# Windowed attention on one core: TensorE's 32 written-out units turned into one loop with hand-made semaphores and single q, k, v buffers

## Chip, cores and metric

The kernel runs on one core of one Trainium2 chip. The metric is the device time of one execution in microseconds (us). Kernels that were timed in the same rounds ran on the same chip, beside runs of the kernel before.

## The reference, cut

q, k and v are float32 of shape (4, 4096, 1536). Each sequence is cut into windows of 64 rows, and attention is taken inside each window.

```python
def reference(q, k, v):
    B, S, D = q.shape                      # 4, 4096, 1536
    W = 64; nw = S // W; scale = D ** -0.5
    q_w, k_w, v_w = (x.reshape(B, nw, W, D) for x in (q, k, v))
    logits = np.einsum('bnwd,bnud->bnwu', q_w, k_w) * scale
    ...                                    # softmax over the last axis
    out = np.einsum('bnwu,bnud->bnwd', attn, v_w)
    return out.reshape(B, S, D).astype(np.float32)
```

There are 302 MB to read and 100.7 MB to write, and little arithmetic for each byte.

## The kernel before

The 16,384 rows are worked on in 32 units of 512. A unit loads q, k and v (3 MB of float32 each, cast to fp16 on the way in), transposes q and k on TensorE, forms the scores, takes the exponent on ScalarE, multiplies by v, divides by the row sums while copying out of PSUM, and stores 3 MB. Loads and stores are issued by GpSimd, but for the first q and the last three pieces of the output, which SyncE issues. q and k have two buffers and v has three, so loads run two or three units ahead. The last unit is cut into three parts, so that its last pieces are small.

```python
    units = [Unit(i * UR, [(0, 4, 2)]) for i in range(N - 1)]
    units.append(Unit((N - 1) * UR, [(0, 2, 2), (2, 3, 1), (3, 4, 1)]))
    qkp = ctx.enter_context(tc.tile_pool(name="qkp", bufs=2))
    vp = ctx.enter_context(tc.tile_pool(name="vp", bufs=3))
    outp = ctx.enter_context(tc.tile_pool(name="outp", bufs=3))
    ...
    for ui, u in enumerate(units):
        for i in range(len(u.parts)):
            last = ui == N - 1 and i == len(u.parts) - 1
            blocks = scores(u, i)              # transposes, products, exponent
            if i == 0:
                load_all(ui + 2, "qk")         # two units ahead
            for h, et in blocks:
                values(u, i, h, et, last)
            if not last:
                store(u, i)
        load_all(ui + 3, "v")                  # three units ahead
```

All of this is written out by Python: TensorE's program holds 32 copies of a unit.

The softmax here doesn't subtract the row's maximum and nothing guards it: scores larger than these inputs give would overflow.

## Time and profile before

| | before |
|---|---|
| time, median (3 runs) | 947.19 us (946.93 to 947.67) |
| span of the profiled run | 945.3 us |
| busy: TensorE, VectorE, ScalarE | 70%, 33%, 34% |
| DMA, software queue | 100.3% of 16 engines' span |

Lines of the profile page of the kernel before. The row of slices gives the busy share of 40 equal slices in tenths; the queue lines give packets, MB and the share of 16 DMA engines' span.

```profile
span 945.3 us, 10170 instructions
PE 662.5 (70%) x4088; PEld 449.4 (48%) x4088; DVE 315.2 (33%) x554; ACT 318.6 (34%) x612; POOL 83.7 (9%) x139
...
DMA  9999999999999999999999999999999999999997
...
q0 software_dynamic: 27232, 249.31, 100.3%
...
q8 instruction: 32, 0.52, 0.2%
q14 instruction: 15, 0.12, 0.0%
HBM read 301.99 MB, written 100.66 MB: 426 GB/s over the span
```

The DMA engines never rest until the last slice, and no compute engine is close to full. So the run is bound by moving bytes. Two more views of the same run follow. First, the waits of TensorE for loads (total, times, longest); then the order in which GpSimd issues its transfers after the first prefetch (start, duration, and in brackets the idle time of GpSimd before it and what ended it).

```profile
PE tp L147 <- DMA q<-in_q_dram: 70.7, 28, 3.8
PE tp L147 <- DMA k<-in_k_dram: 70.5, 30, 3.2
```

```profile
24.89 0.55 POOL L80 DMA_DIRECT2D q<-in_q_dram  x1 [19.41 <-PE tp L147]
31.74 0.54 POOL L80 DMA_DIRECT2D k<-in_k_dram  x1 [6.30 <-PE tp L147]
44.13 0.71 POOL L225 DMA_DIRECT2D out_dram<-out_sb  x1 [11.84 <-DVE xq L151]
44.83 0.72 POOL L80 DMA_DIRECT2D v<-in_v_dram  x1
```

q and k of unit 2 are issued at 25 and 32 us, long before the seven transfers of the start have landed (the last at 55 us).

A reading comes from the trace's completion records. A transfer is spread over 16 DMA engines, and each reports when it is done. The lag of an engine is how much later than the first of the 16 it reports. The engines drift apart:

```
kernel before         first of 16   last of 16   spread   sum of the 16 lags
first v (3rd)             24.59        25.41      0.82          4.6
61st transfer            448.27       451.76      3.49         25.9
119th transfer           871.17       876.90      5.73         45.2
last store               937.53       943.00      5.47         45.6
```

### The profile page before, as it was taken

To read this page: it belongs to the slowest core of one execution; us is meant where nothing else is said; L and a number is where in the kernel's file an instruction comes from. 1 tells how busy PE (TensorE), PEld (TensorE's weight loads), DVE (VectorE), ACT (ScalarE), POOL (GpSimd) and SP (SyncE) were. 2 spreads that over 40 slices of the span, in tenths; PEclk is the share of its full clock that TensorE was granted. 3 is DMA by queue.
4 is the path that set the end of the run, shared out by engine and by line. 5 is a ranking of instruction groups with operands and counts; after the bars stand their busy time and mean duration, and the time that the engine had idled before them with its cause. 6 is when DMAs were issued, how large, how long until landed. Compare 5 with 4: busy or idle time off the path is not lost. (4 is left out here: it accounts for less than half of the span.)

```text
span 945.3 us, 10170 instructions
## 1 busy us (share of the span) xinstructions
PE 662.5 (70%) x4088; PEld 449.4 (48%) x4088; DVE 315.2 (33%) x554; ACT 318.6 (34%) x612; POOL 83.7 (9%) x139
## 2 busy tenths in 40 slices
PE   2877777577766776767777677776677767676673
PEld 1555555345543544535455444554445534455442
DVE  2443234332333332333323333233332333332332
ACT  2443332333323332233332333323333233332342
POOL 1110010100101001010010100110100101001010
PEclk9998898998889999898987899798998798988998
DMA  9999999999999999999999999999999999999997
GB/s 260 216 228 267 281 281 281 242 258 283 282 281 253 247 282 283 280 263 240 280 282 279 273 236 274 282 282 276 240 266 283 280 278 248 255 283 281 281 251 325
DMA packets 27855, 253.89 MB, mean 269 GB/s; under 512 B 2208, under 2 KB 2208, under 8 KB 11808
## 3 DMA queue, kind: packets, MB, share of 16 engines
q0 software_dynamic: 27232, 249.31, 100.3%
q1 hardware_dynamic: 576, 3.93, 1.1%
q8 instruction: 32, 0.52, 0.2%
q14 instruction: 15, 0.12, 0.0%
HBM read 301.99 MB, written 100.66 MB: 426 GB/s over the span
## 5 line engine op out<-in xcount | busy, mean ns | idle before, releaser
L207 PE MATMUL o<-v,et 128*128 128x512 f16 x762 | 202.3, 377 | 50.6 <-ACT out_sb L216 34.2
L161 PE MATMUL lt<-xq,xk 128*128 128x256 f16 (+1 forms) x1536 | 225.7, 298 | 6.4 <-DVE xk L151 6.3
L147 PE MATMUL tp<-ident,q 128*128 128x128 f32 x768 | 142.6, 340 | 101.7 <-DMA q<-in_q_dram 70.7
L147 PE MATMUL tp<-ident,k 128*128 128x128 f32 x768 | 133.3, 312 | 72.3 <-DMA k<-in_k_dram 70.5
L161 PEld LDWEIGHTS <-xk 128*128 128x128 f16 x1536 | 155.5, 105 | 52.3 <-DVE xk L151 17.6
L147 PEld LDWEIGHTS tp<-ident,q 128*128 128x128 f32 x768 | 107.5, 173 | 143.3 <-issue 101.1
L216 ACT ACTIVATE out_sb<-o,rs 128x512 f32<-128x512 f32 x193 | 125.5, 685 | 101.5 <-PE o L207 100.7
L151 ACT COPY xk<-tp 128x512 f32<-128x512 f32 (+1 forms) x96 | 58.6, 610 | 275.2 <-PE tp L147 275.2
L151 DVE COPY xk<-tp 128x512 f32<-128x512 f32 (+1 forms) x97 | 66.9, 690 | 246.5 <-PE tp L147 246.5
L147 PEld LDWEIGHTS tp<-ident,k 128*128 128x128 f32 x768 | 106.4, 162 | 84.2 <-issue 77.0
L218 DVE TENSOR_SCALAR out_sb<-o,rs 128x512 f32<-128x512 f32 x191 | 137.6, 748 | 25.9 <-PE o L207 19.4
L151 DVE COPY xq<-tp 128x512 f32<-128x512 f32 (+1 forms) x129 | 86.7, 687 | 107.1 <-PE tp L147 104.2
L207 PEld LDWEIGHTS <-et 128*128 128x128 f16 x762 | 62.0, 96 | 112.8 <-issue 60.0
L187 ACT ACTIVATE et<-lt,zeros 32x128 f16<-32x128 f32 (+1 forms) x256 | 91.6, 358 | 35.3 <-PE lt L161 29.6
L151 ACT COPY xq<-tp 128x512 f32<-128x512 f32 x64 | 39.0, 609 | 189.3 <-PE tp L147 189.3
L211 DVE RECIPROCAL rs<-sp 128x1 f32<-128x1 f32 x128 | 21.6, 168 | 223.7 <-PE sp L205 223.7
L205 PE MATMUL sp<-ones,et 128*128 128x1 f16 x254 | 42.4, 167 | 40.6 <-ACT et L187 40.6
L205 PEld LDWEIGHTS <-et 128*128 128x128 f16 x254 | 24.4, 96 | 91.5 <-ACT et L187 50.1
L225 POOL DMA_DIRECT2D out_dram<-out_sb x33 | 23.2, 703 | 368.0 <-issue 331.2
L80 POOL DMA_DIRECT2D k<-in_k_dram x34 | 18.5, 544 | 307.6 <-PE tp L147 254.9
L80 POOL DMA_DIRECT2D q<-in_q_dram x33 | 17.9, 541 | 164.5 <-PE tp L147 144.1
L80 POOL DMA_DIRECT2D v<-in_v_dram x34 | 24.0, 708 | 6.6 <-DMA k<-in_k_dram 6.6
(12 smaller groups left out, 7.7 us busy)
## 6 DMA issues: line engine op xcount, KB each, us to landing
out_dram<-out_sb POOLq DMA_DIRECT2D x31, 3072.0 KB, 44.5
k<-in_k_dram POOLq DMA_DIRECT2D x31, 1536.0 KB, 49.6
v<-in_v_dram POOLq DMA_DIRECT2D x31, 1536.0 KB, 51.1
q<-in_q_dram POOLq DMA_DIRECT2D x30, 1536.0 KB, 52.9
raw<-in_q_dram SPq DMA_DIRECT2D x1, 3072.0 KB, 15.5
out_dram<-out_sb POOLq DMA_DIRECT2D x1, 1536.0 KB, 14.2
v<-in_v_dram POOLq DMA_DIRECT2D x1, 768.0 KB, 47.6
v<-in_v_dram POOLq DMA_DIRECT2D x2, 384.0 KB, 46.2
```

The lines of the kernel that those rows point to most:

```text
L80: nc.gpsimd.dma_start(out=dst, in_=rows(src, u.first[i], hi - lo, r))
L147: nc.tensor.transpose(tp[:, (c - c0) * R + r, j, :], pairs[:, c * P : (c + 1) * P], ident)
L151: copy(out=dst, in_=tp)
L161: nc.tensor.matmul(lts[h][:, r, :, :], lhsT=kc[:, r, h, :, w], rhs=qc[:, :, h, :, w], start=(c == 0 and w == 0 and r == 0), stop=(c == DC ...
L187: nc.scalar.activation(et[s, :, :, s], lts[h][s, :, :, s], EXP, bias=zeros[s], scale=scale)
L205: nc.tensor.matmul(sp[:, t, 0:1], lhsT=w, rhs=ones[:, 0:1], start=first, stop=done)
L207: nc.tensor.matmul(os[j], lhsT=w, rhs=u.v[:, lo + R * h + r, 512 * j : 512 * (j + 1)], start=first, stop=done,)
L211: nc.vector.reciprocal(out=rs[:, t : t + 1], in_=sp[:, t, 0:1])
L216: nc.scalar.activation(dst, os[j], COPY, bias=0.0, scale=rs[:, t : t + 1])
L218: nc.vector.tensor_scalar_mul(dst, os[j], scalar1=rs[:, t : t + 1])
L225: nc.gpsimd.dma_start(out=rows(of, u.first[i], hi - lo, R), in_=slots(u.o, lo, hi, R))
```

## The change

The intent was to take TensorE's instruction fetches off the DMA engines and to cut overheads: one loop body for TensorE that fits in one fetch block, semaphores that work as tokens (taken by decrement, so that the body is the same in each turn), weights loaded once for four products, and single q, k and v tiles at fixed addresses, as a loop needs. Refills wait until the tile has been read. The first units are loaded into staging tiles and copied by VectorE. The last unit is no longer cut in parts.

```diff
-    qkp = ctx.enter_context(tc.tile_pool(name="qkp", bufs=2))
-    vp = ctx.enter_context(tc.tile_pool(name="vp", bufs=3))
+    q16 = sb("q16", [P, SLOTS, D], FP16)
+    k16 = sb("k16", [P, SLOTS, D], FP16)
+    v16 = sb("v16", [P, SLOTS, D], FP16)
+    vs = sb("vs", [P, SLOTS, D], FP16)
 ...
+        with nc.Fori(0, N, engines=OrderedEngineSet([PE]), head_slot={PE: 0}):
+            tensor_unit()
+        for u in range(N):
+            vector_unit(u)
+            scalar_unit(u)
 ...
+    def vector_unit(u):
+        for g in range(0, 2 * DC, 2):          # g < 6: q, g >= 6: k
+            copy_out(ve, ve.tensor_copy, u, g)
+            if g == DC - 2:                    # after the last copy of q's transposes
+                src = {1: staged(1, 0), 2: vs, N - 1: vs}.get(u)
+                if src is not None:
+                    ve.wait_ge(*((d_v1, 16) if u == 1 else (d_vs, 16 if u == 2 else 32)))
+                    ...
+                    ve.tensor_copy(out=v16[:, :, :], in_=src[:, :, :]).then_inc(g_v, 1)
 ...
+        for u in range(1, N):                  # GpSimd
+            if u + 1 < N:
+                gp.wait_ge(p_t[1], 6 * u + 3)  # q of unit u transposed
+                load("q", u + 1, q16, d_q)
+                gp.wait_ge(p_t[1], 6 * u + 6)  # k of unit u transposed
+                load("k", u + 1, k16, d_k)
+            if u + 1 == N - 1:
+                load("v", u + 1, vs, d_vs)
+            store(u - 1)
+            if 2 < u + 1 < N - 1:
+                gp.wait_ge(p_o[0], 6 * u + 6)  # values of unit u done
+                gp.wait_ge(p_o[1], 6 * u + 6)
+                load("v", u + 1, v16, d_v)
```

SyncE waits for each landing and hands a token to TensorE. The whole stands in one critical section; a second one clears the semaphores.

## The prediction

> **What bounds the kernel now.** The DMA engines. The page's 40 slices show DMA at 90% or more in all but the last; the queue table gives the software queue 100.3% of the span. TensorE is busy 70%, VectorE 33%, ScalarE 34%. In the list of waits TensorE waits 70.7 us for q, 70.5 us for k. The change keeps every byte (302 MB read, 100.7 MB written). In the packet records of the trace 16 or more packets are in flight from about 3 us to 937 us. One unit's three loads and one store take about 29.4 us of that (945.3 us / 32), while TensorE needs only about 22.7 us (timeline, unit 0 to unit 1, no data wait). So TensorE work saved in mid-run is worth nothing.
>
> **What can be gained.** Queue 8 fetched 32 instruction packets of 16 KB, one per unit, each 0.89 to 0.98 us on one DMA engine. The Trainium skill ("Runtime: NRT & Kernel Launch", Terms) says instruction memory is refilled in 16 KiB blocks; the trace agrees. The fetches fall unevenly: the spread between the first and last of a transfer's 16 completions grows from 0.8 us (first loads) to 5.75 us near the end. Fast engines finish the last stores at 937 us, slow ones at 943 us. One loop in one block removes these fetches; I expect about 4 us back.
>
> **Single buffers.** Stepping the transfers in queue order at 7.4 us each, mid-run stays full: when v lands, the next q, k and a store are already queued (22 us). The two ends are tighter.
> - Start: q and k of unit 2 now wait for unit 1's transposes (before: issued at 24.9 and 31.7 us). Three whole-tile VectorE copies (q, k, v from staging) come before them. I take 1.7 us each, an estimate from "VectorE: DVE Perf Modes", "What auto-detection actually checks" (16-bit SBUF copy, 4 per cycle); the trace has only a float32 cast, 0.92 us per 1536 elements, so 3.7 us at that rate. The 54 us of prefetched transfers are then just met: 0 to 4 us idle.
> - End: VectorE waits in the last unit for v before copying k's transposes. After v lands: copy 1.7, transposes and products 8.2, exponent 1.2, three quarters of the values 6.0 us, then the first half store can be issued. The two older stores cover 14.7 us, so DMA idles about 5 us (more if issue-to-first-packet is long: the first load took 4.5 us). The old split last unit had none.
>
> **Removed from TensorE.** 24 of 32 weight loads per unit in the value stage (0.1 us each): off the critical path.
>
> **Sum.** 947.2 - 4.5 (fetches) + 5 (end) + 1.5 (start) + 0.5 (final semaphore clear) = about 949.5 us. Range 942 to 959. Chances: faster by over 2%: 0.01; within 2%: 0.95; slower by over 2%: 0.04.
>
> **What would show it right.** DMA row still 9 in all middle slices; mean unit period about 29.3 us; no 16 KB packets per unit; spread of completions staying near 1 to 2 us; TensorE still waiting for q, k and v; DMA below 16 in flight near 53 to 90 us and for some 5 us after about 925 us.
>
> **What would make it wrong.** No holes at the ends: then about 943 us. Slow copies or a slow issue path: several us more at both ends. A hole that recurs each unit (the loop's block being fetched again, or a refill coming late through SyncE's relays) multiplies by 32: 1 us each would cost 3%.

## More of the kernel before

At the end, the last GpSimd store is issued at 930.13 us, while transfers still fill the queue.

Most transfers complete about 7.3 us after the one ahead of them.

## The result, and the profile after

The changed kernel took 961.84 us (median of 4 runs, 960.28 to 962.97), the kernel before 947.28 us in the same rounds. The ratio is 1.0152, with a 95% interval from 1.0135 to 1.0170. Where the text takes a difference of medians to the changed kernel, the two were mostly not timed in the same rounds, and the ratios are the safer measure. The sign was as forecast, but the loss is six times the 2.3 us foreseen, and the time lies outside the range.

Lines of the profile page of the changed kernel, answering to those of before:

```profile
span 960.4 us, 10207 instructions
PE 627.1 (65%) x4096; PEld 348.2 (36%) x3328; DVE 300.8 (31%) x524; ACT 341.0 (36%) x643; POOL 82.8 (9%) x133
...
DMA  9999999999999999999999999999999999999993
...
q0 software_dynamic: 26496, 249.31, 99.0%
...
q14 instruction: 16, 0.13, 0.0%
q8 instruction: 2, 0.03, 0.0%
HBM read 301.99 MB, written 100.66 MB: 419 GB/s over the span
```

The 32 fetches of 16 KB have become two, weight loads fell from 449 to 348 us, and the middle of the run is as full as it was (share 1.02 in both, below). So the mechanism in mid-run is as forecast: single buffers cost nothing there, and the time saved on TensorE does not show. The next view is a table of windows of the changed kernel (start and end in us, width, busy time and instructions of each engine, granted clock, DMA share, GB/s).

```profile
53.00:56.00 3.00, 2.48 (x20) 2.04 (x19) 2.16 (x3) 0.63 (x2) 0.99 (x1) 0.87 0.93 135
77.00:80.00 3.00, 1.80 (x17) 1.50 (x15) 2.19 (x3) 0.62 (x1) 1.24 (x1) 1.00 1.04 279
100.00:900.00 800.00, 539.36 (x3532) 298.21 (x2882) 247.39 (x436) 288.77 (x550) 70.26 (x112) 0.90 1.02 269
930.00:946.00 16.00, 12.79 (x87) 6.49 (x62) 4.11 (x8) 7.31 (x15) 0.57 (x1) 0.97 0.36 153
946.00:954.00 8.00, 0.46 (x3) 0.00 (x0) 1.58 (x3) 0.69 (x1) 0.54 (x1) 0.84 0.92 369
```

Of the kernel before, the same view has:

```profile
100.00:900.00 800.00, 574.03 (x3516) 391.20 (x3517) 266.03 (x462) 266.90 (x516) 68.19 (x110) 0.89 1.02 270
930.00:936.00 6.00, 2.58 (x22) 1.56 (x22) 1.67 (x4) 2.56 (x6) 0.54 (x1) 1.00 0.99 421
936.00:944.00 8.00, 0.00 (x0) 0.00 (x0) 0.00 (x0) 0.00 (x0) 0.00 (x0) 0.51 0.50 200
```

From 930 to 946 us the changed kernel's DMA share is 0.36: about 10 us of idle DMA for the average engine. At 53 us only 135 GB/s move although packets are open: the queue has just run dry, and the next packets of 12,288 bytes take up to 2.3 us, where such a packet of a q or k load usually takes 0.93 us.

Set side by side, the completion records split the loss of 15.1 us between the two profiles. The figures are for the slowest of the 16 engines, which ends the run.

```
                                        before     after   difference
122nd transfer, last completion         898.82    903.66      +4.8
from there to the last completion        44.18     50.30      +6.1
from the last completion to the end       2.3       6.5       +4.2
```

(The first 122 transfers are whole ones in both kernels.) Already at the 14th transfer the difference is 5.6 us, so the first line arises at the start, and mid-run gives back at most 0.8 us.

**The start.** The timeline of the changed kernel, ScalarE and TensorE when the first q has landed, then GpSimd's issues:

```profile
16.59 1.28 ACT L322 ACT_TABLE_LOAD   x1 [16.59 <-DMA out<-in_q_dram]
17.88 2.84 ACT L322 CAST q<-out 128x1536 f16<-128x1536 f32 x2
20.80 5.83 PE L139 MATMUL tp<-ident,q 128*128 128x128 f32 x24 [20.80 <-SPq L334]
```

```profile
52.63 1.36 POOL L107 DMA_DIRECT2D q<-in_q_dram  x1 [46.93 <-PE tp L139]
59.58 0.54 POOL L107 DMA_DIRECT2D k<-in_k_dram  x1 [5.58 <-PE tp L139]
60.16 0.71 POOL L289 DMA_DIRECT2D out_dram<-out  x1
76.46 1.78 POOL L107 DMA_DIRECT2D q<-in_q_dram  x1 [15.59 <-PE tp L139]
83.83 0.53 POOL L107 DMA_DIRECT2D k<-in_k_dram  x1 [5.59 <-PE tp L139]
```

q of unit 2 is issued at 52.6 us, where the last prefetched transfer lands between 54.0 and 55.2 us. q of unit 3 comes at 76.5 us and again finds the queue nearly dry. The packet records from 54 to 104 us show two parts of the loss: 1.1 us of idle DMA (at 54 to 56 and 78 to 81 us; 0.0 in the kernel before), and packets that took longer than 0.93 us, whose excess sums to about 3.7 us for the average engine (0.8 before). The share of 1.04 at 77 us hides this, since a slow packet counts as busy. The chain is later than I had put it: the table load, which before ran at 0.74 us, now stands between q and its cast, TensorE waits for all four casts, and the values of unit 0 begin at 36.8 us in place of 34.4.

**The end.** The timeline of the last unit in the changed kernel:

```profile
919.73 0.61 ACT L206 COPY xk<-tp 128x512 f32<-128x512 f32 x1 [1.26 <-PE tp L139]
925.54 1.76 DVE L232 COPY v<-vs 128x6144 f16<-128x6144 f16 x1 [7.42 <-DMA vs<-in_v_dram]
927.22 0.68 DVE L206 COPY xk<-tp 128x512 f32<-128x512 f32 x1
928.05 1.08 PE L139 MATMUL tp<-ident,k 128*128 128x128 f32 x4 [8.36 <-DVE xk L206]
...
944.58 0.57 POOL L372 DMA_DIRECT2D out_dram<-out  x1 [29.05 <-PE o L114]
947.04 0.54 POOL L376 DMA_DIRECT2D out_dram<-out  x1 [1.89 <-PE o L114]
```

VectorE stands 7.4 us before the copy of v, TensorE 8.4 us behind it, and the first half store is issued at 944.58 us. The older stores had been finished by the fastest engine at 934.2 us and by the slowest at 940.5 us.

**The close.** This is from the trace's records of drain instructions, which the profile's views leave out:

```
before: GpSimd drain  930.11 to 944.55, last completion of a transfer 943.00
after:  GpSimd drain  954.25 to 958.56 (4.31 us), last completion 953.96
```

Before, the drain waited beside the transfers. After, it starts only when SyncE has seen every store.

### The profile page after: what moved, and what is told of

Its sections match the earlier page's. It is cut to its first block, busy times and chain, and to the rows that moved or that the text cites. A ratio compares the mean times of both kernels' runs of the same rounds, so it can differ in the third digit from the quotient of the medians.

```text
span 960.4 us, 10207 instructions
## 1 busy us (share of the span) xinstructions
PE 627.1 (65%) x4096; PEld 348.2 (36%) x3328; DVE 300.8 (31%) x524; ACT 341.0 (36%) x643; POOL 82.8 (9%) x133
## 5 line engine op out<-in xcount | busy, mean ns | idle before, releaser
L114 PE MATMUL o<-v,et 128*128 128x512 f16 x768 | 255.0, 451 | 208.9 <-PEq L178 153.8
L279 ACT ACTIVATE out<-o,rs 128x512 f32<-128x512 f32 x192 | 127.1, 686 | 273.3 <-DVE rs L240 195.2
L155 PE MATMUL lt<-xq,xk 128*128 128x256 f16 x1536 | 195.8, 275 | 0.0
L181 PEld LDWEIGHTS <-et 128*128 128x128 f16 x256 | 28.9, 113 | 414.7 <-issue 409.1
L155 PEld LDWEIGHTS lt<-xq,xk 128*128 128x128 f16 x1536 | 148.9, 97 | 23.4
L249 DVE TENSOR_SCALAR out<-o,rs 128x512 f32<-128x512 f32 x192 | 138.4, 748 | 16.8 <-PE o L114 10.5
L206 ACT COPY xk<-tp 128x512 f32<-128x512 f32 x96 | 58.9, 614 | 166.4 <-PE tp L139 166.4
L265 ACT ACTIVATE et<-lt,zeros 32x128 f16<-32x128 f32 x256 | 91.7, 358 | 56.2 <-PE lt L155 53.0
L206 DVE COPY xk<-tp 128x512 f32<-128x512 f32 x96 | 66.4, 692 | 118.6 <-PE tp L139 118.6
L206 DVE COPY xq<-tp 128x512 f32<-128x512 f32 x96 | 66.1, 689 | 56.9 <-PE tp L139 56.9
## 6 DMA issues: line engine op xcount, KB each, us to landing
out<-in_k_dram POOLq DMA_DIRECT2D x1, 1536.0 KB, 36.8
```

The lines of the kernel that those rows point to most:

```text
L114: return nc.tensor.add_instruction(mybir.InstMatmult(name=nc.get_next_instruction_name(), engine=PE, ins=[low(rhs), low(w)], outs=[low(o)] ...
L155: ins = nc.tensor.matmul(lts[h][:, r, :, :], lhsT=halves(xk, c)[:, r, h, :, w], rhs=halves(xq, c)[:, :, h, :, w], start=(c == 0 and w == 0 ...
L181: ld = nc.tensor.ldweights(w)
L206: copy(out=dst, in_=tps[g % 2][:, :, :, :]).then_inc(f_c[g % 4], 1)
L249: ve.tensor_scalar_mul(scaled(u, n, j), ops[j][:, :], scalar1=rs[:, n : n + 1]),
L265: ins = sc.activation(ets[h][s, :, :, s], lts[h][s, :, :, s], EXP, bias=zeros[s, :], scale=scale)
```

## Experiments

Thirteen kernels were run, with five rounds each. All results were correct. The theory: the loss is the sum of a start whose refills come late, a wait for v in the last unit, and a late closing drain, while the fetches gain little because they are not what holds back the slowest engine. The rivals: the fetch saving is real and something larger hides it; the holes are absorbed elsewhere; the loop itself costs something.

### e1_unrolled: TensorE's loop written out again

```diff
-        with nc.Fori(0, N, engines=OrderedEngineSet([PE]), head_slot={PE: 0}):
-            tensor_unit()
         for u in range(N):
+            tensor_unit()
             vector_unit(u)
```

> Only the TensorE loop is undone: the same body is written out 32 times, so the 32 instruction packets of 16 KB return. Theory of the prediction (the fetches delay the slowest DMA engine, and with it the end): 4 us longer than the changed kernel, about 966 us. Rival (the slowest engine of the changed kernel lags for another reason, and the hole at the end lets every engine catch up): within 1 us of 961.8 us, although the sum of the 16 completion lags of a late store goes from 24 us back to 40 us or more. A loop that cost something by itself at each turn would show as a shorter time here.

Measured: 962.80 us (961.87 to 963.60), ratio 1.0168 (1.0154 to 1.0182), against 1.0152 for the changed kernel. The rival held. The 32 packets of 16 KB on queue 8 are back, which shows that they are TensorE's, and the sum of lags of the 119th transfer is 46.6 us, where the changed kernel has 22.9. But the spread is 6.06 us, where the changed kernel has 5.79. With the loop, eleven of the 16 engines stay within 0.72 us of the first at that transfer, against five within 0.51 us here; four lag by 2.6 to 4.2 us, and one as far as without the loop. The hole at the end hides any such lag: the transfer after it has a spread of 0.2 us in both kernels. A cost of the loop by itself doesn't show.

### e2_end: no wait for v in the middle of the last unit's scores

```diff
-            if g == DC - 2:
+            if g == (2 * DC - 2 if u == N - 1 else DC - 2):
```

> In the last unit alone, VectorE copies v out of its staging tile after the six copies of k's transposes, not before five of them... that is, it no longer waits for v in the middle of the score stage. Theory (this wait makes the hole at the end): the first half store is issued about 9 us earlier (near 935.5 us in place of 944.6 us), the hole all but closes, and the run takes 5.5 us less, about 956 us. The DMA share between 934 and 946 us goes from 0.2 to 0.9. Rival (the last unit is limited by the arrival of v itself, or by SyncE's and GpSimd's order): 0 to 2 us less.

Measured: 954.73 us (954.20 to 956.57), ratio 1.0084 (1.0070 to 1.0098). That is 7.1 us less than the changed kernel's median. The expectation's first sentence counts five copies behind the wait; in fact three of VectorE's copies of k's transposes follow it. GpSimd's issues and the window of the end in this run:

```profile
934.08 0.57 POOL L372 DMA_DIRECT2D out_dram<-out  x1 [19.39 <-PE o L114]
936.55 0.55 POOL L376 DMA_DIRECT2D out_dram<-out  x1 [1.89 <-PE o L114]
```

```profile
930.00:936.00 6.00, 4.63 (x24) 0.48 (x5) 2.88 (x7) 2.28 (x5) 0.57 (x1) 1.00 0.85 362
936.00:946.00 10.00, 0.00 (x0) 0.00 (x0) 1.19 (x2) 0.54 (x1) 0.55 (x1) 0.62 0.74 300
```

The half store is issued 10.5 us earlier. The slowest engine finishes the older stores at 939.05 us and everything at 946.49 us, 7.4 us later, which is just the length of the last unit's store: for that engine the hole is closed. For the average engine it is not quite: the shares are 0.85 and 0.74, where 0.9 was expected. The theory of the end is shown.

### e3_store_first: the ready store ahead of the late loads

```diff
         for u in range(1, N):
+            if u <= 3:
+                store(u - 1)
             if u + 1 < N:
 ...
-            store(u - 1)
+            if u > 3:
+                store(u - 1)
```

> In units 1 to 3 GpSimd issues the store of the unit before ahead of the loads of q and k, not behind them. The store is ready at about 47 us, so the queue always holds a transfer while q and k wait for the transposes. Theory (the start costs 4.4 us because freed single buffers are refilled late while a store that is ready stands behind them in GpSimd's order): no slice below full DMA at 53 us and 77 us, and 4 us less, about 958 us. Rival (the start holes are absorbed later, in the slack of a run that is bound by other things): 0 to 1 us less.

Measured: 962.43 us (961.08 to 963.71), ratio 1.0159 (1.0145 to 1.0173): no gain. The windows show why:

```profile
53.00:56.00 3.00, 2.16 (x21) 1.80 (x19) 1.62 (x3) 0.62 (x1) 0.44 (x1) 1.00 0.98 295
77.00:80.00 3.00, 1.27 (x7) 1.30 (x8) 0.91 (x2) 0.00 (x0) 0.70 (x1) 0.83 1.01 426
97.00:102.00 5.00, 3.47 (x25) 2.05 (x19) 2.87 (x5) 2.07 (x4) 1.43 (x2) 1.00 0.64 103
```

The holes at 53 and 77 us are gone, and one at 97 us has taken their place. A store ahead of k delays k by one transfer, so the values of unit 2 begin at 89.9 us in place of 87.4, and v of unit 3, which may be loaded only after them, is issued at 98.7 us in place of 96.2. My cause for the start was wrong in its form. It is not the order of the issues: before the values of unit 2 end, only 13 transfers are allowed at all, and 13 times 7.3 us reach only to about 97 us. That holds for the first of the 16 engines, which at the 14th transfer is only 0.5 us ahead of the changed kernel and stays so. The slowest is 3.1 us ahead there, but 0.4 us at the 122nd transfer: a lag that grows in mid-run (see "Open" below) eats the rest.

### e4_table: the table load out of the chain

```diff
         nc.scalar.wait_ge(i_d, 5)
+        nc.scalar.copy(out=warm[:, :], in_=zeros[:, :])
```

> One dummy copy of a single column on ScalarE before it waits for the first q, so that its table load of 1.28 us no longer stands between the arrival of q and the casts. Theory (the chain from the first q to the first refills sets the start holes): everything in the first units 1.3 us earlier, 1.3 us less in all, about 960.5 us. Rival (the table load is hidden by the wait for k): no change, within 0.4 us.

Measured: 960.47 us (960.12 to 962.04), ratio 1.0144 (1.0128 to 1.0159). That is 1.4 us less by the medians and 0.8 us by the ratios; the interval includes no change. The direction fits the theory, but the run alone doesn't show it.

### e5_drain: the drain beside the last stores

```diff
         gp.dma_start(out=half[:, 0, :], in_=o[:, R, :]).then_inc(d_l[1], 16)
+        gp.drain()
```

> One drain instruction on GpSimd behind its last store, so that the drain which took 4.31 us at the end of the critical section, after the last transfer had landed, has been done while the last stores were moving. Theory (6.4 us from the last landing to the end of the span, against 2.3 us before, because GpSimd's drain starts only when SyncE has seen every store): the closing drain becomes short and the run takes 3 to 4 us less, about 958.5 us. Rival (a drain costs its 4.3 us whenever it comes first after SyncE's release): no change.

Measured: 958.76 us (957.75 to 959.63), ratio 1.0121 (1.0107 to 1.0136), 3.1 us less. The early drain ran from 946.40 to 954.84 us, and the one at the end of the section took 0.05 us. The theory holds: of the 4.2 us lost at the close, this is 3.

### e8_v3_staged: one more v prefetched

```diff
+    vs3 = sb("vs3", [P, SLOTS, D], FP16)
 ...
         load("v", 2, vs, d_vs)
+        load("v", 3, vs3, d_vs3)
 ...
-                src = {1: staged(1, 0), 2: vs, N - 1: vs}.get(u)
+                src = {1: staged(1, 0), 2: vs, 3: vs3, N - 1: vs}.get(u)
```

(with the tokens and the loop of v's refills moved by one unit)

> v of unit 3 is loaded at the start into a staging tile of its own, so that eight loads are queued at the start and not seven, and the load that waited for the values of unit 2 is no longer needed there; VectorE copies it as it does the others (1.76 us more in unit 3). Theory after the store-first run (the start costs time because too few bytes may be fetched before unit 2's values end: 13 transfers of 7.3 us reach 97 us, and v of unit 3 is issued at 96 to 99 us): one transfer more covers the holes, 4 us less, about 957.5 us. Rival (the holes come from the delay between an issue and its first packet, so each late issue keeps its own hole): 1 to 2 us less.

Measured: 960.67 us (958.34 to 961.66), ratio 1.0140 (1.0125 to 1.0155): 1.2 us less, which the rival had expected. In the trace, v of unit 4 has its last completion at 137.93 us, against 142.44 in the changed kernel, so the start itself gained 4.5 us on the slowest engine in the profiled runs. But by the last store of a whole unit, 3.2 us of that are left (937.35 against 940.54), and the runs show 1.2. One more transfer does cover the holes at 53 and 77 us, as the theory says: the packet records have no idle time from 54 to 104 us, and an excess of slow packets of 0.4 us. Its worth in time is not settled by this run.

### e9_copies_late: all copies of v behind k's copies

```diff
-            if g == DC - 2:
+            if g == 2 * DC - 2:
```

> The copies of v out of staging come after the copies of k's transposes in all three units that have one, units 1, 2 and 31. Theory: the end gains what the end-only run gained (7 us), and the start gains as well, since 1.76 us of VectorE leave the chain of units 1 and 2 and no copy holds up GpSimd's issue of q of unit 2 and 3 (1.37 and 1.78 us in place of 0.54): v of unit 3 is issued some 3 us earlier, 10 us less in all, about 951.5 us. Rival (the copies are hidden at the start): as the end-only run, 954.7 us.

Measured: 956.39 us (953.48 to 956.96), ratio 1.0086 (1.0073 to 1.0099), the same as the end-only run. The rival held. The issues of q did become short, as expected: 0.55 and 0.56 us, where the changed kernel has 1.36 and 1.78 us while VectorE's copy runs. But v of unit 3 is issued only 1.2 us earlier (95.0 us), and the runs show nothing of it: the slowest engine is 2.6 us ahead of the changed kernel at the 14th transfer and 0.2 us behind it at the 122nd.

### e6_all: four mends together

Late copies, the third staged v, the early table load and the early drain.

> The four mends together: copies of v late, v of unit 3 staged, table load early, drain early. Theory (the terms add: end 7, start 4.5 as a whole and no more than the hole, closing drain 3): 14 to 15 us less, about 947 us, that is the kernel before again, since mid-run is bound by the same bytes. If the removed instruction fetches are worth something once no hole hides them, up to 3 us below it, about 944 us.

Measured: 948.22 us (947.46 to 951.68), ratio 1.0021 (1.0007 to 1.0035). By the ratios the mends take back 12.4 us of the 14.4 us (1.0152 less 1.0021, times 947.2). The end-only run takes back 6.4 and the drain 2.9. If the terms add, about 3 us are left for the mends of the start together. DMA is full until the end:

```profile
930.00:936.00 6.00, 1.63 (x8) 0.10 (x1) 1.88 (x4) 1.42 (x3) 1.12 (x2) 1.00 0.97 406
936.00:946.00 10.00, 0.00 (x0) 0.00 (x0) 0.00 (x0) 0.00 (x0) 0.00 (x0) 0.50 0.40 159
```

Its last completion is at 943.14 us, where the kernel before has 943.00. So the mended kernel reaches the old time and doesn't pass it.

### e7_all_unrolled, then e12_loop_again and e13_unrolled_again: what the fetches are worth when nothing hides them

The diff of e7 and e13 to e6 is that of e1. e12 is e6 again.

> The kernel with the four mends, with TensorE's loop written out, so that the 32 fetches of 16 KB return where no hole at the end can hide them. Theory of the prediction (each fetch holds up its DMA engine by about 1 us, four of them fall on the slowest engine): 3 to 4.5 us longer than the four mends with the loop, about 952 us, and the sum of the 16 completion lags of a late store about 45 us in place of 25. Rival (the slowest engine is slow for another reason that the loop leaves in place): within 1 us of 948.2 us.

> The four mends with the loop once more, now on the same chip and in the same rounds as the unrolled one, since the two single measurements (1.0021 and 1.0031 of the kernel before) came from different chips and their intervals overlap. Theory (the fetches cost about 2 us once nothing hides them: the profiles had a last spread of 4.7 us with the loop and 6.6 us without it): 948 us, 2 us less than unrolled. Rival (no effect): the two agree within 0.5 us.

> The four mends, TensorE's loop written out, as the partner of the run above. Theory: about 950.5 us and a last spread near 6.6 us. The prediction's 4 us would make it 952 us. Rival: 948.5 us, as with the loop.

Measured: e7 950.53 us, ratio 1.0031 (1.0018 to 1.0045), on another chip than e6. The last two ran on one chip in the same rounds: with the loop 949.16 us, ratio 1.0017 (1.0003 to 1.0031), and unrolled 950.40 us, ratio 1.0039 (1.0025 to 1.0052). Both pairs give the loop an advantage of 1 to 2 us. The intervals of the ratios touch, but in the last pair, on one chip, no run of the one kernel reaches into the other's (948.24 to 949.71 with the loop, 949.80 to 952.27 without). So the advantage is real there, 1.8 us by the means, and it is not 4.5. The way it comes about is not shown: in the last pair's profiled runs the unrolled kernel even had the smaller spread (4.6 against 6.3 us before the last store), with the larger sum of lags (34.5 against 25.5).

### e10_stores_sync: the four mends, with stores on SyncE's queue

```diff
     def store(u):
-        gp = nc.gpsimd
-        gp.wait_ge(n_e[0], 2 * u + 2)
-        gp.wait_ge(n_e[1], u + 1)
-        gp.dma_start(
+        nc.sync.dma_start(
 ...
                 sy.sem_inc(g_w, 1)
+                store(u - 1)
```

> The four mends, and the stores issued by SyncE on its own queue as soon as a unit's last value is scaled, not by GpSimd behind the loads. In the changed kernel one DMA engine falls behind by 0.16 us a unit, in store packets of 0.474 to 0.493 us where the others need 0.460. Theory (that drift belongs to the software queue's stores): it disappears, the last spread is 2 us less, and the run takes 2 to 3 us less than the four mends, about 945.5 us, faster than both kernels. Rival (the drift belongs to the engine, or stores that share the engines with loads delay q and k): the same or longer, 948 to 952 us.

Measured: 964.89 us (964.12 to 966.20), ratio 1.0192 (1.0178 to 1.0206), 17 us more than the mended kernel. The drift of the slowest engine did not get the chance to show. A store and a load in flight together share the engines, so from about 145 us on, q and v of each unit complete some 11 us after the load before them, with a store beside. The loads that TensorE waits for come later (v of the last unit has its last completion at 939.8 us, against 920.8 us in e6), and the stores, which before lay behind the last loads as cover for the last unit, are gone when that unit computes:

```profile
950.59 0.57 POOL L374 DMA_DIRECT2D out_dram<-out  x1 [42.08 <-PE o L117]
950.94 1.90 SPq L383 DMA_DIRECT2D out_dram<-out  x3
```

The first half store comes at 950.6 us, while the last older store had its last completion at 943.5 us.

### e11_before_whole_last: the old kernel with its last unit in one piece

```diff
-    units.append(Unit((N - 1) * UR, [(0, 2, 2), (2, 3, 1), (3, 4, 1)]))
+    units.append(Unit((N - 1) * UR, [(0, 4, 2)]))
```

(and two half stores behind the two blocks of values)

> The kernel before, with its last unit in one piece as the change has it, stored in two halves of 1.5 MB from GpSimd. Theory (the hole at the end comes from the wait for v in mid-unit, not from the whole last unit): the scores of the last unit run as soon as k has landed, under two older stores of 14.7 us; 1 to 2 us longer than the kernel before, about 948.5 us. Rival (a whole last unit by itself costs the 5 to 7 us, since nothing can be stored until it is nearly done): about 953 us.

Measured: 953.08 us (951.86 to 953.52), ratio 1.0058 (1.0045 to 1.0072). The rival held: a whole last unit costs the old kernel 5.5 us. The window of its end:

```profile
929.00:939.00 10.00, 7.55 (x51) 4.41 (x50) 3.26 (x7) 5.53 (x13) 0.27 (x1) 1.00 0.30 128
```

Here k is the last load. Its last completion is at 920.68 us, and the first half store is issued at 938.73, 18 us later, while two older stores cover 14.7 us of the slowest engine and end at 929.3 us on the fastest. So a last unit in one piece needs more than two transfers of cover behind its k. The changed kernel has a third, v, behind k; it threw that cover away by waiting for v before going on with k. By this count moving one copy was enough in e2; no run varied the number of transfers behind k by itself.

## Why the prediction was wrong

**Right.** The DMA engines bound the run, in the changed kernel too (share 1.02 from 100 to 900 us). Single buffers cost nothing in mid-run. Saved weight loads, 101 us of them, show no gain, though no run put them back alone. The ratio of 1.0152 lies within the 2% to which I gave a chance of 0.95. The loss arises at the two ends, with the causes named: late refills at the start, and VectorE's wait for v in the last unit. The copies took 1.75 us against an estimate of 1.7.

**Wrong, term by term of the sum** "947.2 - 4.5 (fetches) + 5 (end) + 1.5 (start) + 0.5 (final semaphore clear)" (the terms as written add to 949.7 us):

- *Fetches, -4.5 us.* This is the step that failed in its mechanism. I read the growth of the spread from 0.8 to 5.75 us as the work of TensorE's fetches, and concluded that without them the slowest engine would be as quick as the others. The fetches were there, and removing them halved the sum of the lags (45 to 23 us at the 119th transfer). But the run ends with the slowest engine, and in the changed kernel one engine lags as far without them (5.8 us at that transfer). In the kernel before the reading fits: from 300 us on the slowest lag stands still but for two steps of about 1.1 us (3.5 to 4.6 to 5.7). In the changed kernel it grows by 0.16 us a unit from about 570 us on, with no fetch of TensorE's left. What failed is the step from "no fetches" to "no lag". Writing the loop out changed the time by 1 us, and by 1 to 2 us in the mended kernel. The saving showed in the mean lag, and hardly in the time.
- *Close, +0.5 us.* It measured +4.2 us by the traces. I had thought of the semaphore clear, not of the drain that GpSimd makes here when a critical section closes (4.31 us). The early drain brings 3 us back.
- *Start, +1.5 us (0 to 4).* By the slowest engine 4.8 us were lost before mid-run's end, about 3 us of which the mends regain. I had costed the chain from the old timeline and did not see that the table load and the wait for all four casts enter it. Also, delays do not just use up slack transfer by transfer: the count of transfers allowed before v of unit 3 sets the limit for the first of the 16 engines (e3).
- *End, +5 us.* The mechanism was right and the size nearly so: +6.1 us by the traces, 6.4 us by e2's ratio. From v's last completion to the half store it took 19.1 us, not the 17.1 that I summed: transposes and products took 9.6, not 8.2 us.

The range was too narrow because the terms were summed as if their errors would cancel. All four erred in the same direction, by about 3.5, 3.7, 3.3 and 1 us.

**Open.** Which engine lags in the changed kernel, and why it falls behind by 0.16 us a unit in store packets of 0.474 to 0.493 us where others take 0.460, is not shown; the records don't name the engine, and e10, which should have told, changed too much. But the kept traces narrow it. From 300 to 900 us, the time that store packets took beyond 0.460 us (leaving out those of 0.473 us, which every kernel has) adds up to 0.03 us in the kernel before and 0.1 us in e11. It is 2.5 to 4.6 us in the changed kernel and in all its versions whose stores GpSimd issues, those with the loop written out among them, and e7 ran on the same chip in the same rounds as e11. So the slow packets come with the changed program, and neither with its loop nor with one chip. What the table load and the staged v are each worth is known only together.

No version beat the kernel before: the best, with four mends, is at 1.0017 to 1.0021 of it.

## What to carry to other kernels

In a kernel that is bound by its transfers, ask of each change only when it lets the next transfer be issued, and what lies behind it in the queue as cover: mid-run forgives a late refill, the first and the last unit don't. A wait in program order on a transfer that isn't needed yet throws away the cover that this very transfer provides. When many engines share the work, a saving that lowers the mean lag need not show in the time, since the slowest engine ends the run and may be slow for another reason. And a close that was hidden beside the last transfers must be checked for staying hidden.

## What the Trainium skill lacked or had wrong

- "Runtime: NRT & Kernel Launch", Terms, says that instruction memory is refilled in 16 KiB blocks. The trace agrees for TensorE (32 packets of 16,384 bytes, one a unit), but in every run all other packets of instructions were of 8,192 bytes, apart from some of 4 to 40 bytes.
- "DMA: Bandwidth & Descriptors", Queues, rings and completion order, puts refills on the runtime's row 14. Here TensorE's came on queue 8: 32 with the program written out, 2 with the loop. Only the smaller ones were on queue 14. This differs from the page only if the profile's queue numbers are the page's rows, which no run shows. The page doesn't say what a refill costs a loaded engine: one packet of 16 KB took 0.89 to 0.98 us in the kernel before.
- No page that I found has the cost of a GpSimd drain behind its own transfers: 4.31 us when it started after the last of them had landed, at the end of a critical section, where it delayed the end. Begun earlier, beside them, it ended 1.5 us behind the last completion (954.84 against 953.36 us in e5), and the kernel before has the same 1.5 us.
- "SBUF — State Buffer", SBUF: two separate sides, warns that a VectorE copy in a two-port mode keeps GpSimd from writing descriptors. The trace agrees: issuing a load took 1.36 and 1.78 us while the copy ran, against 0.54 us. The page sizes the effect for another case only. The run that removed the collision (e9) gained nothing measurable.
- "VectorE: DVE Perf Modes", What auto-detection actually checks, was right for the fp16 copy: 6144 elements a partition in 1.75 us.
- No page gives a size for how unequal the 16 engines become in a long run: the spread of one transfer's completions, at the 122nd, was 4.2 to 7.4 us in these runs.
